# All convolution taps on TensorE, from copies by VectorE and ScalarE, with the mixer's products in a new order

## The chip, the cores and the metric

The kernel runs on one core of a Trainium2 chip. The metric is the device time of one execution in microseconds (us); a run's time is that of the whole program, and the figures of a kernel are the median of its runs. A profile is one execution, recorded instruction by instruction on the five engines: TensorE (PE in the rows, PEld its weight loads), VectorE (DVE), ScalarE (ACT), GpSimd (POOL) and SyncE (SP, which here only issues DMAs).

## The reference: what is computed

A decoder trunk of two layers on 256 tokens of 1024 features, in float32: layer 0 is an FFN, a mixer of pooling and convolution, and an FFN; layer 1 an FFN, a sparse attention, and an FFN; each with RMSNorm ahead and a residual sum behind. What the change touches is the mixer of layer 0, cut here to its core:

```python
proj = h @ ab_w_in[i]                                   # 1024 -> 512 + 512 + 512
u_pool, u_val, u_gate = jnp.split(proj, ab_cuts, axis=-1)
y_pool = pool_mixer(u_pool, pool_w[i], pool_scale[i])   # trailing means over 2, 4, 8, 16 tokens
y_conv = conv_module(u_val, u_gate, conv_w[i], ...)
y = jnp.concatenate([y_pool, y_conv], axis=-1) @ ab_w_out[i]

def conv_module(a, gate, conv_w, conv_b, ln_g, ln_b):
    z = a * jax.nn.sigmoid(gate)
    z = causal depthwise conv of z, width 31, over the tokens, + conv_b
    mu, var = mean and variance of z over the 512 channels
    return jax.nn.silu((z - mu) * lax.rsqrt(var + NORM_EPS) * ln_g + ln_b)
```

Each of the 512 channels has 31 taps of its own: output token t is the sum over n of w[n, channel] * z[t - 30 + n, channel].

## The kernel before, in words

Products of float32 accuracy are made of three fp32r products, high x high, high x low and low x high. So every weight goes through three steps: SP loads it (`raw`, L147), ScalarE rounds it (`hi`, L160), and one engine subtracts (`lo = raw - hi`, L184). `pump(n, eng)` does this for the next n weights of a list that is fixed ahead, in the order of their use; `eng` says which engine subtracts, VectorE unless GpSimd (`pool`) is named, and None shares one weight between the two. A weight of kind "gu" is 1024 x 256 (1 MB, two pieces in every step), one of kind "d" 128 x 1024 (512 KB). Rounded and subtracted weights stand in three buffers of kind "gu" and five of kind "d"; a load is issued when a raw buffer is free.

The program is written out by hand: there is no scheduler, and each engine runs its instructions in the order in which the code issues them. So a line in `mixer_ab` that is moved moves on every engine that it uses.

`mixer_ab` runs after the first FFN, whose tail hands over the normalised, transposed tokens `hT` (the second token tile's transposes are done by `finish_b`, inside `wide`). Features are on the partitions, the 256 tokens in the columns, so a block is 128 channels. It goes through:

- Projections: `wide` makes three weights' products (value and gate of channel blocks 0 to 2), `project` the others one by one: block 3, pooling groups 2 and 3, pooling groups 0 and 1. `wide_sum2` (L716, L717) adds the two halves of a result, `glu` (L505, L506) writes z with 30 zero columns ahead into a tile `keep`.
- The convolution, with taps split: 20 of the 31 are done by TensorE, 11 by VectorE. For TensorE, `shift_z` (L541) copies z into four column shifts: for each of four groups of 32 channels a tile whose 128 partitions hold these 32 channels at four neighbouring tokens. It is 16 copies of 32 partitions for each block, some on ScalarE and the rest on VectorE (`COPIES`). `taps_pe` (L548) then makes 20 products of 128 x 32 weights with 256 columns, four taps in each, from a pack (`wd`). The pack holds each tap's weight on a diagonal of 32; `make_pack` (L524) builds it on GpSimd from the small constants `cpk` and a stacked identity `eye`. `taps_dve` (L567 to L576) is a generator: `conv(n)` issues its next n operations on VectorE, each multiplying z, shifted by one token, with a per-channel weight and adding.
- Pooling: `windows` (L598) sums on GpSimd by doubling, `pool_diff` (L620 to L624) subtracts the token on VectorE, `pool_map` multiplies and splits the result (L638 on ScalarE, L639 on VectorE).
- The channel norm: `mean_mm` on TensorE, `squares` (L673, L674), `variance` (L680, with a power on GpSimd), `spread` (L689), and `swish` for each of two token tiles (L703, L705, L699, L700).
- The output: `out_mm(t, k)` (L349) multiplies pooling block k for token tile t; `tail` multiplies the four convolution blocks, adds the residual, normalises and transposes for the next FFN. `load_gain` reads the norm's gain into the tile that shifts 0 and 2 use as well (`gain`).

Line numbers are those of the kernel before.

## Time and profile before

| what | value |
|---|---|
| median of 3 runs | 1007.56 us (1006.82 to 1009.68) |
| the profiled execution | 1007.73 us |
| its span in the profile | 1006.0 us |
| mean granted clock of TensorE | 0.983 |
| TensorE busy | 967.3 us, 96% of the span |
| VectorE busy | 686.3 us, 68% |
| ScalarE busy | 534.8 us, 53% |
| GpSimd busy | 106.9 us, 11% |

The span is what the profile covers, and the execution's time has 1.73 us around it. Busy time of TensorE counts pipelined products, so 96% is not 96% of its peak. A busy share of the whole span says nothing on one stage: the four FFNs take most of it, and the mixer of layer 0, about 200 to 305 us, is read from the timelines of that stage. In a timeline a row can stand for several instructions one behind the other (xcount), and its length is then that of all of them; what stands in brackets is the engine's idle time before the row and what ended it.

### The profile page before, as it was taken

What the parts mean: (1) busy time and instruction counts of PE and PEld (TensorE: products, weight loads), DVE (VectorE), ACT (ScalarE), POOL (GpSimd) and SP (SyncE); (2) the same over time, 40 slices, a digit from 0 to 9 for tenths busy, and PEclk for the clock granted to TensorE, in tenths of its full rate; (3) what the DMA queues carried; (4) which work ended last, traced back from release to release, by engine and by line L of the source; (5) the groups of instructions that cost most, each with busy time, mean ns of one, the idle gap of its engine ahead of it and who ended that gap; (6) DMA issues with size and microseconds to landing.
All of it is one profiled execution on the core that took longest, in us unless ns stands there. A gap on an engine that the chain in (4) does not pass through costs nothing.

```text
span 1006.0 us, 14588 instructions
## 1 busy us (share of the span) xinstructions
PE 967.3 (96%) x5642; PEld 839.0 (83%) x5642; DVE 686.3 (68%) x1107; ACT 534.8 (53%) x961; POOL 106.9 (11%) x116
## 2 busy tenths in 40 slices
PE   7999999978499999999999999999999999999997
PEld 7888888868279888888888888888889898888885
DVE  6876666689976866665676666657888758666653
ACT  5665555455245755555466555545466646555542
POOL 4000000064520010000000000000344100000000
PEclk9999999998889999999999999999999999999999
DMA  8765555432333756655455555445454526655401
GB/s 334 275 251 188 188 189 189 167 115 85 103 128 110 267 209 235 235 208 188 151 208 223 188 189 189 158 167 188 174 175 158 189 85 230 216 192 192 175 2 42
DMA packets 37460, 179.98 MB, mean 179 GB/s; under 512 B 6352, under 2 KB 6384, under 8 KB 24208
## 3 DMA queue, kind: packets, MB, share of 16 engines
q1 hardware_dynamic: 32400, 169.92, 47.0%
q0 software_dynamic: 4704, 8.88, 2.8%
q8 instruction: 44, 0.72, 0.3%
q10 hardware_dynamic: 288, 0.27, 0.1%
q14 instruction: 24, 0.20, 0.1%
HBM read 177.89 MB, written 4.22 MB: 181 GB/s over the span
## 4 chain that ended last, share of the span: by engine, by line
PE 85%; DVE 10%; issue 2%; ACT 1%; DMA 1%; POOL 0%; SPq 0%; POOLq 0%; DVEq 0%; ACTq 0%
PE g L292 28%; PE g L295 15%; PE a L349 14%; PE b L349 12%; PE g L276 4%; PE g L320 2%; PE g L323 2%; DVE zq L541 1%; PE g L312 1%; DVE odd L569 1%; DVE t L569 1%; DVE lo L184 1%; PE a L323 1%; PE a L320 1%; PE b L869 1%
## 5 line engine op out<-in xcount | busy, mean ns | idle before, releaser
L184 DVE TENSOR_TENSOR lo<-raw,hi 128x1024 fp32r<-128x1024 f32 (+1 forms) x308 | 367.3, 1244 | 53.9 <-ACT hi L160 53.9
L160 ACT CAST hi<-raw 128x1024 fp32r<-128x1024 f32 x320 | 314.9, 1043 | 4.8 <-DMA raw<-in_c_out 2.4
L292 PE MATMUL g<-hT,hi 128*128 128x512 f32 x1248 | 310.7, 391 | 0.8 <-DVE t L335 0.8
L292 PEld LDWEIGHTS g<-hT,hi 128*128 128x128 f32 x1248 | 228.7, 188 | 44.8 <-DVE t L335 1.0
L332 ACT COPY t<-g 128x256 f32<-128x256 f32 x174 | 63.3, 371 | 220.6 <-PE g L295 205.1
L295 PEld LDWEIGHTS g<-hT,lo 128*128 128x128 f32 x1248 | 170.3, 190 | 12.2
L295 PE MATMUL g<-hT,lo 128*128 128x256 f32 x1248 | 174.0, 282 | 0.0
L335 DVE TENSOR_TENSOR t<-g,t 128x256 f32<-128x256 f32 x174 | 71.8, 421 | 137.8 <-ACT t L332 137.8
L349 PE MATMUL a<-hi,kh 128*128 128x512 f32 x208 | 83.3, 401 | 0.1
L349 PE MATMUL b<-hi,kh 128*128 128x512 f32 x208 | 83.0, 399 | 0.0
L349 PE MATMUL a<-lo,kh 128*128 128x512 f32 x208 | 82.3, 396 | 0.0
L349 PE MATMUL a<-hi,kl 128*128 128x512 f32 x208 | 81.3, 391 | 0.7 <-DVE kl L639 0.7
L349 PE MATMUL b<-hi,kl 128*128 128x512 f32 x208 | 81.5, 392 | 0.0
L349 PE MATMUL b<-lo,kh 128*128 128x512 f32 x208 | 81.5, 392 | 0.0
L243 POOL TENSOR_TENSOR sm<-sm,mhalf 128x1 f32<-128x1 f32 x11 | 6.1, 555 | 659.8 <-DVE sm L241 659.8
L398 ACT CAST kh<-t 128x256 fp32r<-128x256 f32 x88 | 35.8, 406 | 57.9 <-DVE t L396 57.9
L399 DVE TENSOR_TENSOR kl<-t,kh 128x256 fp32r<-128x256 f32 x88 | 37.5, 426 | 41.6 <-ACT kh L398 41.6
L276 PE MATMUL g<-hT,hi 128*128 128x256 f32 x320 | 45.9, 300 | 8.6 <-DVE t L717 8.6
L394 ACT ACTIVATE t<-t 128x256 f32<-128x256 f32 x88 | 37.1, 422 | 26.8 <-DVE t L335 26.8
L276 PEld LDWEIGHTS g<-hT,hi 128*128 128x128 f32 x320 | 42.5, 204 | 10.0 <-DVE t L717 9.1
L349 PEld LDWEIGHTS a<-hi,kl 128*128 128x128 f32 x208 | 39.4, 189 | 10.0 <-DVE kl L639 1.1
L349 PEld LDWEIGHTS b<-hi,kl 128*128 128x128 f32 x208 | 39.3, 189 | 8.4
(214 smaller groups left out, 1032.5 us busy)
## 6 DMA issues: line engine op xcount, KB each, us to landing
raw<-in_gu SPq DMA_DIRECT2D x87, 1024.0 KB, 4.8
raw<-in_dn SPq DMA_DIRECT2D x88, 512.0 KB, 5.5
raw<-in_c_qk SPq DMA_DIRECT2D x8, 1024.0 KB, 5.7
raw<-in_ab_in SPq DMA_DIRECT2D x6, 1024.0 KB, 4.9
raw<-in_ab_out SPq DMA_DIRECT2D x8, 512.0 KB, 5.2
raw<-in_c_v SPq DMA_DIRECT2D x8, 512.0 KB, 4.2
raw<-in_c_out SPq DMA_DIRECT2D x8, 512.0 KB, 4.2
eall<-escr POOLq DMA_DIRECT2D x4, 768.0 KB, 17.0
```

Of the source, the lines that this page charges most:

```text
L160: act.copy(hi[:, c], raws[k][:, c])
L184: e.tensor_tensor(lo[:, c], raws[k][:, c], f32(hi[:, c]), op=ALU.subtract)
L276: pe.matmul(dst, wt[:, c, cols], hT[:, c, part, :], start=n == 0, stop=n == len(seq) - 1)
L292: pe.matmul(b, hi[:, c, cols], hT[:, c, 0:2, :], start=c == 0, stop=False, skip_group_check=True)
L295: pe.matmul(b[:, 0:256], lo[:, c, cols], hT[:, c, 0, :], start=False, stop=c == NCH - 1, skip_group_check=True)
L320: pe.matmul(bv[:, :, P:2 * P], w[0][:, c, cs], hT[:, c, 0:2, P:2 * P], start=False, stop=False, skip_group_check=True)
L332: act.copy(t[:m], bv[:, 1, :])
L335: dve.tensor_tensor(dst[:m], bv[:, 0, :], t[:m], op=ALU.add)
L349: pe.matmul(acc, kt[a][:, ts], w[b][:, hs], start=start and n == 0, stop=stop and n == 2)
L394: act.activation(s, gv, AF.Silu)
L398: act.copy(hi, m)
L399: dve.tensor_tensor(lo, m, f32(hi), op=ALU.subtract)
```

## The change

All 31 taps go to TensorE, filled up to 32, so that a pack holds eight rounds of four taps instead of five. The packs are laid out on the host as an input `cpack` (four of 128 x 1024 fp32) and loaded by GpSimd's DMA queue: packs 0 and 1 at the eighth hidden block of the first FFN, 2 and 3 inside the mixer, when the two pack buffers come free. `taps_dve`, `make_pack` and `eye` are gone; one VectorE operation (`taps_out`) adds the bias to TensorE's sum. Six of every 16 shift copies are on ScalarE, ten on VectorE, 284 columns wide instead of 272. Window sums and all subtractions of weights in the mixer are on VectorE; GpSimd keeps memsets, DMA issues and the powers. `wide` uses each of its three results at once and pumps a weight behind each. The lines of `mixer_ab` from the projections on are written in a new order.

```diff
-ROUNDS = 5
-PE_TAPS = 4 * ROUNDS
-DVE_TAPS = TAPS - PE_TAPS
-ZW = 252 + PE_TAPS
-COPIES = (7, 6, 9, 4)
+ROUNDS = 8
+ON_ACT = 6
+ZW = 256 + 4 * (ROUNDS - 1)
...
+    def load_pack(j):
+
+        dg = tpool.tile([P, 4 * ROUNDS, 32], F32, tag="wd", name=nm("wd"), bufs=2)
+        pool.dma_start(dg, d["cpack"][j])
+        packs[j] = dg
+
     def mixer_ab(finish_b, gname):
...
-        def make_pack(j, eng):
-            n = PE_TAPS
-            dg = tpool.tile([P, 32 * PE_TAPS], F32, tag="wd", name=nm("wd"), bufs=3)
...
-                    n_act = COPIES[j]
-                    on_act = (4 * i + q + 1) * n_act // 16 > (4 * i + q) * n_act // 16
+                    on_act = (4 * i + q + 1) * ON_ACT // 16 > (4 * i + q) * ON_ACT // 16
...
-        def taps_dve():
...
+        def taps_out(j):
+            ys[j] = t1()
+            dve.tensor_scalar(ys[j], where[j][:, 0:256], convb[:, j:j + 1], None, op0=ALU.add)
+
...
-                pool.tensor_tensor(s2[:, 2 * n - 1:272], s[:, 2 * n - 1:272],
-                                   s[:, n - 1:272 - n], op=ALU.add)
+                dve.tensor_tensor(s2[:, 2 * n - 1:272], s[:, 2 * n - 1:272],
+                                  s[:, n - 1:272 - n], op=ALU.add)
...
         def use(bvs):
-            wides.append([(bv[:, 0, :], bv[:, 1, :]) for bv in bvs])
-            if len(wides) == 1:
-                glu(0, *[wide_sum2(hi, lo) for hi, lo in wides[0]])
+            val, gt = [wide_sum2(bv[:, 0, :], bv[:, 1, :]) for bv in bvs]
+            glu(len(items), val, gt)
+            items.append(True)
...
-        wide([(weights("gu"), list(zip(two, t)), use) for t in tags], finish_b, False, AHEAD)
-        pump(1, pool)
-        pump(1, pool)
-        conv(14)
+        wide([(weights("gu"), list(zip(two, t)), use) for t in tags], finish_b, True, AHEAD)
         taps_pe(0, "b0")
-        glu(1, *[wide_sum2(hi, lo) for hi, lo in wides[1]])
-        glu(2, *[wide_sum2(hi, lo) for hi, lo in wides[2]])
-        conv(5)
-        pump(1, pool)
-        conv(6)
-        v3 = project("g1")
-        glu(3, *v3)
-        pump(1, dve)
+        taps_out(0)
+        load_pack(2)
+        glu(3, *project("a0"))
         taps_pe(1, "b1")
-        conv(13)
+        taps_out(1)
+        load_pack(3)
         p23 = project("a1")
         windows(2, p23)
-        make_pack(3, pool)
+        taps_pe(2, "b0")
+        taps_out(2)
+        pump(1)
+        g = load_gain(gname)
         pool_diff(2)
-        g = load_gain(gname)
+        taps_pe(3, "g1")
+        mean_mm((0, 1, 2))
+        pump(1)
+        taps_out(3)
         preload(AF.Silu)
         p01 = project("g0")
+        mean_mm((3,))
+        pool_map(2, "g3")
+        squares()
         windows(0, p01)
-        taps_pe(2, "b0")
-        conv(6)
-        pump(1, None)
-        pool_map(2, "g3")
-        taps_pe(3, "g1")
-        pump(1, pool)
+        variance(0, "g1")
+        out_mm(0, 0)
+        out_mm(1, 0)
+        variance(1, "g2")
         pool_diff(0)
-        pump(1, pool)
-        out_mm(0, 0)
-        conv(7)
-        mean_mm((0, 1, 2))
-        pool_map(0, "g3")
+        out_mm(0, 1)
         out_mm(1, 1)
-        conv(5)
-        out_mm(0, 1)
-        out_mm(1, 0)
+        pool_map(0, "g0")
+        spread(0, "g3")
+        spread(1, "g1")
+        pump(1)
+        swish(0)
         out_mm(0, 2)
-        pump(1, None)
-        pump(1, dve)
-        mean_mm((3,))
-        squares()
-        out_mm(1, 2, (1,))
-        out_mm(1, 2, (0,))
-        variance(0, "g1")
-        variance(1, "g3")
+        out_mm(1, 2)
+        pump(1)
         out_mm(0, 3)
-        spread(0, "g1")
-        pump(1, None)
-        swish(0)
-        spread(1, "g0")
+        out_mm(1, 3)
         swish(1)
-        out_mm(1, 3)
+        pump(2)
...
-    pool.tensor_tensor(eye, ident[:, 0:32], ident[:, 32:64], op=ALU.add)
-    for q in (64, 96):
-        pool.tensor_tensor(eye, eye, ident[:, q:q + 32], op=ALU.add)
-    fb = ffn(0, None, "mxn0", first=first)
+    fb = ffn(0, None, "mxn0", first=first, extra=lambda: (load_pack(0), load_pack(1)))
```

The instruction order at three places, of the kernel before first and of the changed kernel second. In the rows, names have buffer numbers; `t` are work tiles, `a`, `b` and `g` PSUM banks, `hi` and `lo` a weight's rounded and subtracted part, `wd` a pack, `gain` and `zq` the shifted copies, `kh` and `kl` the parts of a block for the output product. Line numbers of the changed kernel are its own (its L182 is the subtraction, L528 the shift copy, L535 the taps, L268 a projection, L620 the mean, L587 the pool map).

VectorE, from the first channel block's gate on. Before:

```order
L506 TENSOR_TENSOR keep_1940<-t_399_2083,t_397_2077 128x256
L541 COPY gain_2086<-keep_1940 32x272 x9
L567 TENSOR_SCALAR t_407_2183<-keep_1940,cpk 128x256
L567 TENSOR_SCALAR odd<-keep_1940,cpk 128x256
L569 SCALAR_TENSOR_TENSOR t_407_2183<-keep_1940,cpk,t_407_2183 128x256
L569 SCALAR_TENSOR_TENSOR odd<-keep_1940,cpk,odd 128x256
```

Changed:

```order
L507 TENSOR_TENSOR keep_1940<-t_398_2080,t_396_2074 128x256
L528 COPY gain_2083<-keep_1940 32x284 x10
L182 TENSOR_TENSOR lo_2103<-raw_1710,hi_2100 128x1024 x2
L670 TENSOR_TENSOR t_403_2140<-g_381_1974,t_403_2140 128x256
L670 TENSOR_TENSOR t_404_2143<-g_382_1983,t_404_2143 128x256
L507 TENSOR_TENSOR keep_1943<-t_405_2146,t_403_2140 128x256
L528 COPY zq_2149<-keep_1943 32x284 x5
L528 COPY zq_2150<-keep_1943 32x284 x5
```

Where the eleven taps of block 0 and their sum stood behind the nine copies, the fourth projection's weight (`raw_1710`) is subtracted, which GpSimd did before; the sums and copies of block 1 follow at once.

TensorE, from the last projection on (before), and from the end of the last taps on (changed). Before:

```order
L276 MATMUL g_448_2486<-hT,hi_2276 128x256 x16
L276 MATMUL g_448_2486<-hT,lo_2279 128x256 x8
L276 MATMUL g_448_2486<-hT,hi_2276 128x256 x16
L276 MATMUL g_448_2486<-hT,lo_2279 128x256 x8
L548 MATMUL b_454_2547<-gain_2253,wd_1953 32x256 x20
L634 MATMUL g_459_2583<-t_442_2472,pw 128x256
L634 MATMUL g_459_2583<-t_444_2477,pw 128x256
L548 MATMUL g_464_2594<-zq_2342,wd_2470 32x256 x2
L548 MATMUL g_464_2594<-zq_2343,wd_2470 32x256 x2
```

Changed:

```order
L535 MATMUL g_448_2507<-zq_2331,wd_2383 32x256 x2
L620 MATMUL g_449_2540<-t_419_2274,ones 128x256
L620 MATMUL g_449_2540<-t_426_2381,ones 128x256
L620 MATMUL g_449_2540<-t_439_2487,ones 128x256
L268 MATMUL g_455_2556<-hT,hi_2233 128x256 x16
L268 MATMUL g_455_2556<-hT,lo_2236 128x256 x8
L268 MATMUL g_455_2556<-hT,hi_2233 128x256 x16
L268 MATMUL g_455_2556<-hT,lo_2236 128x256 x8
L620 MATMUL g_449_2540<-t_453_2552,ones 128x256
L587 MATMUL g_456_2606<-t_444_2497,pw 128x256
```

Before, the last projection (`g_448`) is followed by block 2's taps, the first pool map and block 3's taps; now all taps are ahead of it, three mean products stand between, and the last mean product and the pool map follow it.

VectorE, from the second half of `swish` to the tail's first residual sum. Before:

```order
L700 TENSOR_TENSOR kl_2781<-t_522_2808,kh_2780 128x128
L703 TENSOR_TENSOR t_494_2717<-t_494_2717,g_521_2805 128x128
L700 TENSOR_TENSOR kl_2786<-t_523_2811,kh_2785 128x128
L699 CAST kh_2790<-t_524_2814 128x128
L700 TENSOR_TENSOR kl_2791<-t_524_2814,kh_2790 128x128
L700 TENSOR_TENSOR kl_2798<-t_525_2819,kh_2797 128x128
L235 SCALAR_TENSOR_TENSOR x_87<-a_475_2641,x_87 128x512
L235 SCALAR_TENSOR_TENSOR x_88<-a_476_2642,x_88 128x512
```

Changed:

```order
L653 TENSOR_TENSOR kl_2734<-t_513_2789,kh_2733 128x128
L656 TENSOR_TENSOR t_464_2620<-t_464_2620,g_494_2722 128x128
L653 TENSOR_TENSOR kl_2739<-t_514_2792,kh_2738 128x128
L652 CAST kh_2743<-t_515_2795 128x128
L653 TENSOR_TENSOR kl_2744<-t_515_2795,kh_2743 128x128
L653 TENSOR_TENSOR kl_2751<-t_516_2800,kh_2750 128x128
L182 TENSOR_TENSOR lo_2810<-raw_2493,hi_2808 128x1024
L182 TENSOR_TENSOR lo_2817<-raw_2173,hi_2814 128x1024 x2
L227 SCALAR_TENSOR_TENSOR x_86<-a_477_2662,x_86 128x512
```

Between the last `kl` and the residual sum (`x_86` now, `x_87` before) there are now three subtraction pieces: the last output weight (`lo_2810`) and one weight of the next FFN (`lo_2817`).

## Rows read from the trace of the kernel before

**Rows 1.** The page's slices: TensorE's granted clock, 40 slices, tenths of full speed.

```profile
PEclk9999999998889999999999999999999999999999
```

**Rows 2.** TensorE's timeline: start, length, line, out<-in, count, [idle before, releaser].

```profile
204.58 0.66 PE L253 MATMUL b<-ident,h 128*128 128x128 f32 x4 [1.02 <-DVE h L246]
...
218.59 2.37 PE L548 MATMUL b<-gain,wd 128*32 128x256 f32 x40
229.53 3.78 PE L276 MATMUL g<-hT,hi 128*128 128x256 f32 x16 [8.57 <-DVE t L717]
...
239.82 2.18 PE L276 MATMUL a<-hT,hi 128*128 128x256 f32 x16
...
245.67 2.08 PE L276 MATMUL g<-hT,hi 128*128 128x256 f32 x16
...
260.48 1.22 PE L634 MATMUL g<-t,pw 128*128 128x256 f32 x2 [6.59 <-DVE t L624]
...
276.35 1.22 PE L634 MATMUL g<-t,pw 128*128 128x256 f32 x2 [5.77 <-DVE t L624]
...
287.24 1.95 PE L680 MATMUL g<-ones,t 128*128 128x1 f32 x16 [0.26 <-ACT t L674]
...
292.36 0.39 PE L349 MATMUL a<-hi,kh 128*128 128x512 f32 x1
...
304.62 3.98 PE L312 MATMUL g<-hT,hi 128*128 128x256 f32 x32
```

**Rows 3.** Table by stretch: length, TensorE busy, granted clock, DMA share, GB/s.

```profile
222.00:224.00 2.00, 0.00 (x0) 0.99 0.41 66
234.00:236.00 2.00, 2.00 (x18) 0.95 0.00 0
```

**Rows 4.** VectorE's timeline of the mixer stage.

```profile
202.10 2.43 DVE L246 SCALAR_TENSOR_TENSOR h<-x,sm,gain 128x512 f32<-128x512 f32 x2 [0.67 <-POOL sm L243]
...
212.34 0.42 DVE L506 TENSOR_TENSOR keep<-t,t 128x256 f32<-128x256 f32 x1 [0.48 <-ACT t L505]
212.86 2.79 DVE L541 COPY gain<-keep 32x272 f32<-32x272 f32 x9
...
217.01 0.48 DVE L569 SCALAR_TENSOR_TENSOR t<-keep,cpk,t 128x256 f32<-128x256 f32 x1
217.41 2.63 DVE L569 SCALAR_TENSOR_TENSOR odd<-keep,cpk,odd 128x256 f32<-128x256 f32 x1
...
242.16 11.34 DVE L541 COPY zq<-keep 32x272 f32<-32x272 f32 x12
253.53 1.23 DVE L184 TENSOR_TENSOR lo<-raw,hi 128x1024 fp32r<-128x1024 f32 x1
...
269.16 2.62 DVE L620 SCALAR_TENSOR_TENSOR t<-t,t 128x256 f32<-128x256 f32 x1
...
286.51 1.66 DVE L673 TENSOR_TENSOR t<-t,g 128x128 f32<-128x128 f32 x8
...
290.94 0.68 DVE L703 TENSOR_TENSOR t<-t,g 128x128 f32<-128x128 f32 x3 [0.69 <-PE g L689]
...
293.76 0.49 DVE L700 TENSOR_TENSOR kl<-t,kh 128x128 fp32r<-128x128 f32 x2
```

**Rows 5.** GpSimd's timeline of the same stage.

```profile
202.26 4.61 POOL L524 TENSOR_TENSOR wd<-cpk,eye 128x640 f32<-128x640 f32 x3
...
217.03 10.19 POOL L184 TENSOR_TENSOR lo<-raw,hi 128x1024 fp32r<-128x1024 f32 x4 [9.58 <-ACT hi L160]
...
246.50 4.94 POOL L598 TENSOR_TENSOR t<-t 128x271 f32<-128x271 f32 x7
...
269.14 9.45 POOL L184 TENSOR_TENSOR lo<-raw,hi 128x1024 fp32r<-128x1024 f32 x4 [3.87 <-ACT hi L160]
```

**Rows 6.** ScalarE's timeline: its copies for the first shift.

```profile
212.84 3.02 ACT L541 COPY gain<-keep 32x272 f32<-32x272 f32 x7 [0.54 <-DVE keep L506]
```

**Rows 7.** DMA issues, 200 to 310 us: count, KB each, median us to landing.

```profile
gain<-in_f2n POOLq DMA_DIRECT2D x1, 512.0 KB, 4.5
```

More of the change, by code (lines that the diff above doesn't have):

```diff
@@ L206, in tile_trunk @@
     pool.memset(mhalf, -0.5)
-    cpk = cpool.tile([P, 32 + 4 * TAPS], F32, name="cpk")
+    cpk = cpool.tile([P, 32], F32, name="cpk")
     convb, lng, lnb, pscale = (cpk[:, 4 * i:4 * i + 4] for i in range(4))
     rcount = cpk[:, 16:32]
-    convw, packw, o = [], [], 32
-    for j in range(4):
-        convw.append(cpk[:, o:o + DVE_TAPS])
-        packw.append(cpk[:, o + DVE_TAPS:o + TAPS])
-        o += TAPS
-    eye = cpool.tile([P, 32], F32, name="eye")
     escr = dpool.tile([16, 384], F32, name="escr")
@@ L500, in mixer_ab @@
             pool.memset(z[:, 0:30], 0.0)
+            pool.memset(z[:, 286:288], 0.0)
             zs.append(z)
@@ L550, in taps_pe @@
                               stop=m == ROUNDS - 1, skip_group_check=True)
-        def taps_dve():
-            for j in range(4):
-                while j not in ready_z:
-                    yield False
-                z = zs[j]
-                ys[j] = y = t1()
-                sums = [y, odd]
-                for n in range(DVE_TAPS):
-                    acc = sums[n % 2]
-                    zk, wk = z[:, PE_TAPS + n:PE_TAPS + n + 256], convw[j][:, n:n + 1]
-                    if n == 0 and j in where:
-                        dve.scalar_tensor_tensor(acc, zk, wk, where[j][:, 0:256],
-                                                 op0=ALU.mult, op1=ALU.add)
-                        added.add(j)
-                    elif n < 2:
-                        dve.tensor_scalar(acc, zk, wk, None, op0=ALU.mult)
-                    else:
-                        dve.scalar_tensor_tensor(acc, zk, wk, acc, op0=ALU.mult, op1=ALU.add)
-                    yield True
-                dve.scalar_tensor_tensor(y, odd, convb[:, j:j + 1], y, op0=ALU.add, op1=ALU.add)
-                yield True
-                if j not in added:
-                    while j not in where:
-                        yield False
-                    dve.tensor_tensor(y, where[j][:, 0:256], y, op=ALU.add)
-                    added.add(j)
-                    yield True
-        odd = spool.tile([P, 256], F32, name="odd")
-        gen = taps_dve()
-        def conv(n):
-            for _ in range(n):
-                if not next(gen, False):
-                    return
-        for j in range(3):
-            make_pack(j, pool)
+        def taps_out(j):
+            ys[j] = t1()
+            dve.tensor_scalar(ys[j], where[j][:, 0:256], convb[:, j:j + 1], None, op0=ALU.add)
         pw = tpool.tile([P, 512], F32, tag="h", name="pw", bufs=4)
@@ L604, in new_u @@
             u = t15()
-            pool.memset(u[:, 0:16], 0.0)
+            dve.memset(u[:, 0:16], 0.0)
             return u
@@ L1190 @@
     rcount = np.broadcast_to(1.0 / np.arange(1, 17, dtype=np.float32), (P, 16)).astype(np.float32)
+    arrays["cpk"] = np.concatenate(cols + [rcount], axis=1)
+    pack = np.zeros((4, 4, 32, 4, ROUNDS, 32), np.float32)
     for j in range(4):
-        own, n = cw[:, P * j:P * j + P], PE_TAPS
-        cols.append(own[n:].T)
-        cols.append(own[:n].reshape(n // 4, 4, 4, 32).transpose(1, 3, 2, 0).reshape(P, n))
-    arrays["cpk"] = np.concatenate(cols[:4] + [rcount] + cols[4:], axis=1)
+        own = np.zeros((4 * ROUNDS, P), np.float32)
+        own[:TAPS] = cw[:, P * j:P * j + P]
+        own = own.reshape(ROUNDS, 4, 4, 32)
+        for c in range(32):
+            pack[j, :, c, :, :, c] = own[:, :, :, c].transpose(1, 2, 0)
+    arrays["cpack"] = pack.reshape(4, P, 4 * ROUNDS, 32)
     arrays["rel_bias"] = z["rel_bias"]
```

11 lines of the change are left out of this document (2 added, 9 removed).

## The prediction

> **What bounds the kernel now.** I read the page's slices of the span first: TensorE's granted clock shows 9 in every slice but three, slices 10 to 12 of 25 us each, about 226 to 302 us [rows 1]. That is the convolution mixer of layer 0, where nearly all of the change lies, so the rest of the walk is this one stage. TensorE's timeline of the stage comes next: the reader is to see what stands in brackets behind a row. It sat idle for 1.02, 8.57, 6.59 and 5.77 us, each time released by VectorE [rows 2]; smaller waits add some 1.2 us. The clock table then shows what an idle costs behind its end: still 0.99 of full speed at 222 to 224 us, 3 us into the idle that began at 221.0, half speed after that, and full again only at about 234.1, 4.6 us after work had resumed at 229.53 [rows 2, 3]. Work at 1.2 GHz instead of 2.4 lost about 2.3 us there, and the two later idles lost about as much each, some 7 us in all. So VectorE ends last and TensorE waits: of the 101.7 us between the second token tile's transposes and the next FFN's first product (202.9 to 304.62) about 30 are idle time or half speed.
>
> Why VectorE is late stands in its own timeline, read beside GpSimd's. A tap of 256 columns takes 0.48 us at 217.01 and 2.63 at 217.41 [rows 4]; GpSimd began four subtraction pieces at 217.03 and worked on them for 10.19 us [rows 5]. Twelve shift copies took 11.34 us from 242.16, where nine took 2.79 from 212.86; GpSimd's seven window sums ran from 246.50 to 251.4. One operation of pool_diff took 2.62 us at 269.16, and GpSimd had begun at 269.14. The normalisation's two products at 202.10 took 2.43 beside the packs that GpSimd made from 202.26 [rows 4, 5]. VectorE stands nearly still exactly while GpSimd computes.
>
> **The change part by part.** It takes GpSimd's tensor work out of this stage (four packs, 13 subtraction pieces, ten window sums), takes 44 tap operations off VectorE, gives VectorE the subtractions and window sums, gives TensorE 32 taps for each block of 128 channels instead of 20, and puts the products in another order. I lay the new order on the old time axis, with the old durations.
>
> *TensorE, first part.* The wait of 1.02 goes with the packs, so the first three projections end at 218.59 - 1.02 = 217.57. One block's taps cost 2.37 x 32/20 = 3.79; a projection costs 245.67 - 239.82 = 5.85 [rows 2]. In the new order: taps 0 to 221.36, projection to 227.21, taps 1 to 231.00, projection to 236.85, taps 2 to 240.64, taps 3 to 244.43, then the last projection and six 256-column fp32 products (four for the mean, two of the pool map). One such product took 1.22 at half speed, so 0.6 at most at full speed; back to back I take 0.3. That gives 244.43 + 5.85 + 1.8 = 252.1. The extra taps, 4 x 1.42 = 5.7 us, are all on the path.
>
> *Does VectorE keep up?* One projected block costs it two sums and the gate with ScalarE's sigmoid between, 1.8; ten copies at 2.79/9 = 0.31, 4% wider, 3.2; two subtraction pieces at 1.2 (a piece of that size: 1.23), 2.4; and 0.4 in which it waits for ScalarE's rounding. Sum 7.8. The first block's copies end at 215.1 (from 209.3, with 2.6 for its sums), its subtractions at 217.9, the second block's at 225.8, the third's at 233.6 [rows 4]. One output (0.4), the fourth gate (0.4) and ten more copies: 237.7 with its waits for ScalarE. Needed: the third block's copies at 236.85 against 230.9, the fourth's at 240.64 against 237.7. ScalarE's six copies (seven took 3.02 [rows 6]) end before VectorE's ten and cost nothing. Next come seven window sums, which VectorE has not run here. Bounds: 0.42, its sum of two SBUF tiles of 256 columns, and GpSimd's 4.94/7 = 0.71 [rows 4, 5]; I take 0.5, nearest to VectorE's own row: 241.6. With pool_diff, two outputs and three subtraction pieces it reaches 247.5; the last mean product is due at 251. VectorE has 2 to 3 us of slack throughout and is hidden by TensorE.
>
> *TensorE, second part.* From 252.1 short steps follow one another. Two pool-map results are split by ScalarE and VectorE in turn, 4 x 0.5; VectorE starts the squares at 254.2, and the first variance ends 1.7 later (from 286.51 to 287.24 and half of 1.95 [rows 2, 4]): 255.9. TensorE idles for about 2.8 of that. Then 12 output products (at 0.23: the old tail's 48 and two transposes of 0.36 took 304.62 - 292.36), 2.8; a variance, 1.0; 12 more; pool map 0.6; spreads 0.7: 263.7. A wait of 0.5 for the split results and 24 products, 5.5: 269.7.
>
> *A new wait in the tail.* The last two blocks of output weights are now subtracted behind the two swish halves on VectorE. The first swish starts at about 266.8 and takes 3.3 (290.94 to 293.76 + 0.49 [rows 4]): 270.1. With ScalarE's rounding and the subtraction: 271.6. Second swish: 274.9. ScalarE has rounded the last weights by 275.2, VectorE has subtracted them by 276.3. Queued behind that on VectorE are two pieces for the next FFN (2.4), then the residual sum. TensorE is at the tail's first half from 269.7, waits 0.6 for the one and 3.2 and 0.4 for the other, and ends that half at 276.9. Left are 36 products and two transposes, 8.3 + 0.7: 285.9. The old time of that point is 304.62 [rows 2], so 18.7 us are gained. The next FFN's third weights are now subtracted ahead of the second tile's transposed lows; TensorE waits about 0.65 for those. Net 18.05.
>
> A second account: 30 of idle and half speed removed, 5.7 of taps and 8.2 of new waits added, gives 16; the walk stands, and 2 us are its looseness.
>
> *Edits at nothing.* Two packs of 512 KB are loaded at the eighth of the first FFN's 22 hidden blocks, long before use. The other two go out when taps 0 and 1 have freed their buffers, at 221.4 and 231.0. A load of that size landed in 4.5 [rows 7], so they are there at 225.9 and 235.5, needed at 236.85 and 240.64; without that cover each costs what it is late. Behind them on GpSimd's queue stand only a gain load, due some 40 us later, and the rstd powers from 258. The dropped eye operations lie where nobody waits for GpSimd. SP's weight loads keep their order through the eight output blocks and are released no later than before.
>
> **The rivals.** *The clock falls at the new waits.* Idles of 2.8 and 3.2 us follow within 20 us. For: all three old idles of over 5 us ended at half speed. Against: 3 us into the first it was still at 0.99 [rows 3]. Price 2.3 a fall [rows 2, 3]: 992.0 for one, 994.3 for both. Chance 0.18.
>
> *A pack is late.* No row here has a GpSimd DMA issued beside VectorE's copies, so the issue's price there is open. If the fourth pack's issue at 231.0 stands until the copies end at 237.7, it lands at 242.2 and TensorE waits 1.6: 991.3. Chance 0.07. The Trainium skill, "SBUF — State Buffer", section "Who interferes with whom", states such a lock: an fp32 copy within SBUF takes, for the whole instruction, a port pair that GpSimd needs to write a DMA's descriptors. By that rule the sum would be 991.3, by the bare row of the load 989.7; no run here shows which.
>
> *The long VectorE rows were not GpSimd's doing*, and the change does not do what it says. If all 40 copies kept the mean of the slow twelve, 11.34/12 = 0.945 [rows 4], VectorE would lose 40 x 0.63 = 25.2, less 2.9 of slack 22.3: slower than before, 1012. The place is the four series of copies, and it decides from a mean of 0.31 + (18.05 + 2.9)/40 = 0.83 us a copy. With half that excess the time is 999. Against: the starts coincide within 0.4 us in the rows above, and the copies at 212.86, without GpSimd, are fast beside ScalarE's copies of the same tile. Chance 0.03 for slower, 0.04 for the half.
>
> *Less waiting.* If the new waits are hidden (the split chain and the last weights), up to 8.2 more: 981.5 at the bound, 985 in the middle. Chance 0.12.
>
> **How the numbers follow.** The profiled execution took 1007.73 us (span 1006.0, 1.73 around it), close to the median of 1007.56. 1007.73 - 18.05 = 989.7. Chance of that within 3 us: 0.56. The range takes in the less-waiting middle, both clock falls, a late pack, and window sums at 0.71: 983 to 998. About 3 us, 0.3%, is what a measurement of this kernel can tell from no change; of the cases only slow copies come near it. Faster 0.95, same 0.02, slower 0.03.
>
> **What would show it.** In the profile after: no VectorE tap rows; copies of about 0.3 everywhere and no VectorE row of 2 us; taps of 64 TensorE rows in 3.8; the clock full from 200 to 252; TensorE's idles now before the first variance (2.8) and in the tail's first half (3 to 4, released by the weights' halves), and the next FFN's start at about 286 instead of 304.62. Wrong would be a wait for a pack at taps 2 or 3, VectorE as the releaser between 217 and 252, or half speed after the two idles.

## The result, and the profile after

The changed kernel takes 994.94 us (median of 4 runs, 993.01 to 996.05); the kernel before took 1008.05 beside it (4 runs, 1006.82 to 1009.68). The ratio is 0.9866, with an interval of 0.9846 to 0.9886: 13.1 us faster, where 18.05 were predicted. The time lies in the predicted range, 5.2 us above the predicted 989.7. The profiled execution took 993.01 us (span 991.2); it is the fastest of the four, which matters below.

From the page of the changed kernel: busy time of three engines, TensorE's clock in 40 slices, and the shares of the chain that ended last.

```profile
PE 968.1 (98%) x5738; PEld 839.5 (85%) x5738; DVE 657.3 (66%) x1086; ACT 534.0 (54%) x959; POOL 62.9 (6%) x90
...
PEclk9999999999999999999999999999999999999999
...
PE 92%; DVE 3%; issue 2%; ACT 1%; DMA 1%; POOL 0%; SPq 0%; POOLq 0%; DVEq 0%; ACTq 0%
```

The three slices at 8 [rows 1] are gone, GpSimd's busy time fell from 106.9 to 62.9 us, and VectorE's part of the chain, 10% before, is 3%. But a slice is 25 us long and hides what is short. TensorE's timeline of the same stage (start, length, line, out<-in, count, [idle before, releaser]; L535 the taps, L620 the mean, L587 the pool map, L633 the variance, L341 the output products, L304 and L312 the next FFN) answers to [rows 2]:

```profile
217.69 3.66 PE L535 MATMUL b<-gain,wd 128*32 128x256 f32 x64
...
240.25 3.64 PE L535 MATMUL g<-zq,wd 128*32 128x256 f32 x64
...
251.40 1.02 PE L587 MATMUL g<-t,pw 128*128 128x256 f32 x4
255.07 1.05 PE L633 MATMUL g<-ones,t 128*128 128x1 f32 x8 [2.65 <-ACT t L627]
...
260.24 1.13 PE L633 MATMUL g<-ones,t 128*128 128x1 f32 x8
...
273.53 0.50 PE L341 MATMUL a<-lo,kh 128*128 128x512 f32 x1 [0.47 <-DVE lo L182]
...
276.96 0.50 PE L341 MATMUL a<-hi,kh 128*128 128x512 f32 x1 [2.70 <-ACT hi L158]
278.22 0.80 PE L341 MATMUL a<-lo,kh 128*128 128x512 f32 x1 [0.76 <-DVE lo L182]
...
289.24 4.00 PE L304 MATMUL g<-hT,hi 128*128 128x256 f32 x32
...
296.59 1.34 PE L312 MATMUL g<-hT,hi 128*128 128x256 f32 x8 [0.32 <-DVE hT L252]
```

From 200 to 252 us not one row has an idle time in brackets: the old waits of 1.02, 8.57, 6.59 and 5.77 us are gone, and a block's 64 tap instructions (two for each fp32 product) take 3.66. What is left are five waits in brackets: 2.65 before the first variance, 0.47, 2.70 and 0.76 in the tail, 0.32 in the next FFN. The next FFN's first product starts at 289.24 instead of 304.62; predicted was 285.9.

The clock table of the changed kernel shows where most of the missing 3.3 us went (length, then busy time and count of PE, PEld, DVE, ACT and POOL, then TensorE's granted clock, DMA share, GB/s):

```profile
256.00:257.00 1.00, 1.00 (x6) 0.82 (x6) 0.11 (x3) 1.00 (x5) 0.00 (x0) 1.00 0.02 8
257.00:258.00 1.00, 1.00 (x4) 0.84 (x3) 0.00 (x0) 0.00 (x0) 0.00 (x0) 0.60 0.06 16
258.00:259.00 1.00, 1.00 (x4) 0.71 (x4) 0.00 (x0) 0.00 (x0) 0.00 (x0) 0.50 0.00 0
...
260.00:261.00 1.00, 1.00 (x8) 0.91 (x7) 0.25 (x1) 0.00 (x0) 0.00 (x0) 0.69 0.00 0
256.00:264.00 8.00, 8.00 (x34) 6.61 (x34) 2.61 (x14) 1.00 (x5) 1.25 (x2) 0.79 0.01 3
274.00:288.00 14.00, 10.55 (x44) 8.17 (x43) 8.53 (x17) 6.73 (x14) 0.55 (x1) 0.88 0.45 150
```

Work had resumed at 255.07, behind the idle of 2.65 us; 2 us later the clock was still full, then it fell to its lower level (0.50 is 1.2 of 2.4 GHz; 0.60 from 257 to 258 puts the fall at 257.2) and was back at 260.6: 3.4 us at half speed. The same followed the idle of 2.70, from 277.7 to 281.1. The 12 output products between the two variances were predicted at 2.8 us; from the first variance's end (256.12) to the second's start they take 4.1.

VectorE's timeline answers to [rows 4]: shift copies (L528) and window sums (L551).

```profile
211.96 3.18 DVE L528 COPY gain<-keep 32x284 f32<-32x284 f32 x10
...
234.54 3.18 DVE L528 COPY zq<-keep 32x284 f32<-32x284 f32 x10
...
238.37 3.15 DVE L551 TENSOR_TENSOR t<-t 128x271 f32<-128x271 f32 x7
...
260.75 1.34 DVE L551 TENSOR_TENSOR t<-t 128x271 f32<-128x271 f32 x3 [4.64 <-PE g L633]
```

Copies now take 0.3 us everywhere, where the slow twelve took 0.945, and no row of 2 us for one operation is left. The fourth copies end at 237.7, as predicted to the tenth, and the seven window sums take 0.45 each.

### The profile page after: what moved, and what is told of

Read it like the earlier page. It is cut to its first block, busy times and chain, and to the rows that moved or that the text cites. A ratio compares the mean times of both kernels' runs of the same rounds, so it can differ in the third digit from the quotient of the medians.

```text
span 991.2 us, 14724 instructions
## 1 busy us (share of the span) xinstructions
PE 968.1 (98%) x5738; PEld 839.5 (85%) x5738; DVE 657.3 (66%) x1086; ACT 534.0 (54%) x959; POOL 62.9 (6%) x90
## 4 chain that ended last, share of the span: by engine, by line
PE 92%; DVE 3%; issue 2%; ACT 1%; DMA 1%; POOL 0%; SPq 0%; POOLq 0%; DVEq 0%; ACTq 0%
PE g L284 29%; PE g L287 15%; PE a L341 14%; PE b L341 13%; PE g L268 4%; PE g L312 2%; PE g L315 2%; PE g L304 2%; PE a L268 1%; PE b L535 1%; DVE lo L182 1%; PE a L315 1%; PE a L312 1%; PE b L811 1%; DVE keep L957 1%
## 5 line engine op out<-in xcount | busy, mean ns | idle before, releaser
L182 DVE TENSOR_TENSOR lo<-raw,hi 128x1024 fp32r<-128x1024 f32 (+1 forms) x319 | 380.4, 1243 | 56.3 <-ACT hi L158 56.3
L284 PEld LDWEIGHTS g<-hT,hi 128*128 128x128 f32 x1248 | 228.7, 188 | 44.8 <-DVE t L327 1.0
L341 PE MATMUL a<-hi,kh 128*128 128x512 f32 x208 | 83.4, 401 | 2.8 <-ACT hi L158 2.7
L341 PE MATMUL a<-lo,kh 128*128 128x512 f32 x208 | 82.8, 398 | 1.2 <-DVE lo L182 1.2
L341 PE MATMUL b<-hi,kh 128*128 128x512 f32 x208 | 82.3, 396 | 0.0
L341 PE MATMUL a<-hi,kl 128*128 128x512 f32 x208 | 81.8, 393 | 0.0
L341 PE MATMUL b<-hi,kl 128*128 128x512 f32 x208 | 81.5, 392 | 0.0
L341 PE MATMUL b<-lo,kh 128*128 128x512 f32 x208 | 81.5, 392 | 0.0
L341 PEld LDWEIGHTS a<-hi,kh 128*128 128x128 f32 x208 | 39.6, 191 | 10.0 <-ACT hi L158 3.1
L341 PEld LDWEIGHTS a<-hi,kl 128*128 128x128 f32 x208 | 39.5, 190 | 9.0 <-DVE kl L592 0.2
L341 PEld LDWEIGHTS b<-hi,kl 128*128 128x128 f32 x208 | 39.3, 189 | 8.3
L341 PEld LDWEIGHTS b<-hi,kh 128*128 128x128 f32 x208 | 39.4, 189 | 8.2
```

Of the source, the lines that this page charges most:

```text
L182: e.tensor_tensor(lo[:, c], raws[k][:, c], f32(hi[:, c]), op=ALU.subtract)
L284: pe.matmul(b, hi[:, c, cols], hT[:, c, 0:2, :], start=c == 0, stop=False, skip_group_check=True)
L341: pe.matmul(acc, kt[a][:, ts], w[b][:, hs], start=start and n == 0, stop=stop and n == 2)
```

## The experiments

The theory was: VectorE ended last because GpSimd's tensor work stretched its operations and because it had 44 taps to do; with both gone TensorE is full but for short idles, and these cost their length and, as the profile after shows, a stretch at half speed. The rivals: GpSimd's share was nothing or everything; the pack loads cost something; the idles cost only their length. The stage below is the time from the first taps to the next FFN's first product: 86.0 us before (304.62 - 218.59), 71.55 after. (The old wait of 1.02 us, which goes as well, lies ahead of it.) It is a sharper measure than the run's time, since the time at which the stage begins scatters by up to 5 us (last section). The kernel before was run again beside each version, and its median there lay between 1006.49 and 1010.13 us; so ratios compare two versions better than their medians do.

**GpSimd's tensor work alone taken out of the kernel before.** The taps, the packs and the order stay.

```diff
-                pool.tensor_tensor(s2[:, 2 * n - 1:272], s[:, 2 * n - 1:272],
+                dve.tensor_tensor(s2[:, 2 * n - 1:272], s[:, 2 * n - 1:272],
...
-        pump(1, pool)
+        pump(1)
...
-        pump(1, None)
+        pump(1)
```

> The kernel before with one edit: inside the mixer, the 13 subtraction pieces and the ten window sums that GpSimd did are done by VectorE; taps stay 20 on TensorE and 11 on VectorE, the packs are still made on GpSimd, the order of the products is the old one. Theory (GpSimd's tensor work holds VectorE back): VectorE gains back some 27 us of stretched rows and takes on 13 x 1.2 + 10 x 0.45 = 20 us, so the time falls by about 7 us, to 998 to 1004, and no VectorE row of 2 us stands beside GpSimd except at the packs. Rival (VectorE is late by its taps, and the long rows are not GpSimd's doing): 20 us of added work on the engine that is waited for, 1020 to 1028.

Measured: 1001.88 us (1001.27 to 1004.19), ratio 0.9927 [0.9911, 0.9943]. VectorE's timeline of this kernel (L541 copies, L598 window sums):

```profile
246.15 3.65 DVE L541 COPY zq<-keep 32x272 f32<-32x272 f32 x12
...
256.25 3.15 DVE L598 TENSOR_TENSOR t<-t 128x271 f32<-128x271 f32 x7
```

Its TensorE:

```profile
230.12 3.72 PE L276 MATMUL g<-hT,hi 128*128 128x256 f32 x16 [6.99 <-DVE t L717]
...
260.06 2.08 PE L634 MATMUL g<-t,pw 128*128 128x256 f32 x4 [6.10 <-DVE t L624]
...
271.55 1.30 PE L634 MATMUL g<-t,pw 128*128 128x256 f32 x4 [1.95 <-DVE t L624]
```

The twelve copies that took 11.34 us [rows 4] take 3.65, though VectorE now also makes the subtractions and the window sums. So the long rows were GpSimd's doing; the rivals (1012 in the prediction, 1020 to 1028 here) are refuted. But TensorE still waits 6.99, 6.10 and 1.95 us for VectorE, and the stage is 80.8 us (in the slowest of the four executions, which is the profiled one). This part of the change is worth some 7 of its 13 us.

**The new order without GpSimd's work, but with 11 taps of each block back on VectorE.**

```diff
-ROUNDS = 8
+ROUNDS = 5
...
-            dve.tensor_scalar(ys[j], where[j][:, 0:256], convb[:, j:j + 1], None, op0=ALU.add)
+            for n in range(DVE_TAPS):
...
+                    dve.scalar_tensor_tensor(acc, zk, wk, acc, op0=ALU.mult, op1=ALU.add)
```

> The changed kernel with taps split as before: 20 of 31 taps on TensorE (packs of five rounds, copies 272 wide), 11 on VectorE at the place of each block's output; no tensor work on GpSimd, order as changed. Theory (moving taps is the second part of the gain): TensorE has 5.7 us less, VectorE about 18 us more with 2 to 3 us of slack, so TensorE waits for it and the time is 1003 to 1010. Rival (the whole gain is GpSimd's absence and the order): within 2 us of the changed kernel's 994.9, or faster by the 5.7 us of products.

Measured: 1007.74 us (1002.31 to 1009.63), ratio 0.9978 [0.9961, 0.9995]; stage 84.2. The table by stretch (VectorE's busy time is the third behind the length, after PE and PEld):

```profile
230.00:240.00 10.00, 6.73 (x67) 4.00 (x66) 9.66 (x25) 3.54 (x10) 0.54 (x1) 0.93 0.47 159
240.00:250.00 10.00, 4.74 (x40) 3.08 (x38) 9.68 (x28) 4.67 (x6) 0.00 (x0) 0.84 0.00 0
250.00:260.00 10.00, 6.99 (x34) 6.82 (x35) 9.90 (x24) 0.00 (x0) 0.00 (x0) 0.55 0.26 84
```

Two waits of its TensorE (L635 the mean, L648 the variance):

```profile
253.01 1.22 PE L635 MATMUL g<-t,ones 128*128 128x256 f32 x2 [7.31 <-DVE t L556]
...
266.60 1.05 PE L648 MATMUL g<-ones,t 128*128 128x1 f32 x8 [2.65 <-ACT t L642]
```

VectorE is busy 29.2 of 30 us, and TensorE waits for it. The profiled execution took 1002.31 us, the fastest of ten, so the typical stage is longer than 84.2. The new order is made for short work on VectorE; with the taps there it gains next to nothing, and it is some 5 us slower than the old order with the same split in the run above (ratios 0.9978 and 0.9927). So 5.7 us more products on TensorE bought 11 us by the ratios: the order and the place of the taps belong together. The old order with all taps on TensorE was not run, so what the order alone is worth there stays open.

**Subtractions of three projection weights back on GpSimd**, the rest as changed.

```diff
-                pump(1)
+                pump(1, eng)
...
-        wide([(weights("gu"), list(zip(two, t)), use) for t in tags], finish_b, True, AHEAD)
+        wide([(weights("gu"), list(zip(two, t)), use) for t in tags], finish_b, True, AHEAD, pool)
```

> The changed kernel with one edit: the three weights that are subtracted behind the three first projections (six pieces, 7 us of VectorE) are subtracted by GpSimd instead. Theory (GpSimd holds VectorE back): VectorE loses work and gets slower all the same; copies and sums beside GpSimd's pieces take up to 2.5 us, TensorE waits at taps 1 to 3, and the time rises by 5 to 15 us to 1000 to 1010. Rival (only VectorE's own amount of work counts): no slower than the changed kernel, 993 to 996.

Measured: 1004.08 us (1003.15 to 1004.28), ratio 0.9943 [0.9928, 0.9958]; stage 82.6. The time is as the theory has it, but the trace says that most of it came another way. TensorE's wait:

```profile
245.15 5.05 PE L535 MATMUL b<-gain,wd 128*32 128x256 f32 x64 [7.99 <-DVE t L551]
```

And GpSimd's rows (L182 subtractions, L493 the loads of packs):

```profile
234.06 4.78 POOL L182 TENSOR_TENSOR lo<-raw,hi 128x1024 fp32r<-128x1024 f32 x2 [4.27 <-issue]
238.78 1.13 POOL L493 DMA_DIRECT2D wd<-in_cpack  x2
```

The taps at 245.15 read pack 2, and both packs' loads were issued together from 238.78 on, right behind GpSimd's last subtraction; in the changed kernel they go out at 221.69 and 231.25. The row names VectorE's window sums as releaser, which these taps don't read; the two loads took 6.6 us to land (median), and the first landing is about when the taps begin. So this run mixes two prices, and two more runs part them: both leave out the loads of packs 2 and 3, the one without and the other with the subtractions on GpSimd.

```diff
-        load_pack(2)
+        packs[2] = packs[0]
...
-        load_pack(3)
+        packs[3] = packs[1]
```

> The changed kernel, but blocks 2 and 3 use packs 0 and 1 again, so the two packs that are loaded inside the mixer are left out (the weights of those two blocks are not the right ones; every instruction of the engines stays). Theory (the issues on GpSimd's queue beside VectorE's copies cost nothing; they stood 0.53 us each and nobody waited): 994 to 996, stage (first taps to the next FFN's first product) 71 to 72.2 against 71.55. Rival (the issues or the 1 MB of loads slow VectorE's copies): at least 1 us less, copies below 0.29 us each.

> The same without the two packs, and the subtractions of the three projections' weights back on GpSimd, as in e2_subs_on_gpsimd, but now no load can stand behind them. Theory (GpSimd's tensor work slows VectorE by itself, through what the two share): VectorE's fourth copies take 5 to 6 us for ten instead of 3.2 and end at about 241 to 242, although 7 us of work were taken off VectorE; two rows of 2.6 us for one operation beside GpSimd's; TensorE waits 1 to 4 us at the fourth block's taps or the mean; stage 73 to 77, time 996.5 to 1000.5. Rival (all of e2's loss was the packs standing behind the subtractions on GpSimd's queue): no wait of TensorE between 200 and 250 us, stage 71 to 72.2, time as e7_two_packs within 0.7.

Measured: 994.38 us (991.03 to 994.78, ratio 0.9841 [0.9816, 0.9867]) without, and 994.05 (993.37 to 994.81, ratio 0.9849 [0.9832, 0.9866]) with the subtractions on GpSimd. The first is the changed kernel's time within its interval: the two loads cost nothing. Its stage, 74.5 us, misses the expected 71 to 72.2, because half speed behind its two idles lasted longer than in the first profile of the changed kernel (see the changed kernel once more, below). Of the second, VectorE's timeline:

```profile
218.56 2.62 DVE L507 TENSOR_TENSOR keep<-t,t 128x256 f32<-128x256 f32 x1 [0.48 <-ACT t L506]
221.28 3.18 DVE L528 COPY zq<-keep 32x284 f32<-32x284 f32 x10
...
235.79 5.86 DVE L528 COPY zq<-keep 32x284 f32<-32x284 f32 x10
```

GpSimd's:

```profile
216.16 4.74 POOL L182 TENSOR_TENSOR lo<-raw,hi 128x1024 fp32r<-128x1024 f32 x2 [12.70 <-ACT hi L158]
...
234.11 4.81 POOL L182 TENSOR_TENSOR lo<-raw,hi 128x1024 fp32r<-128x1024 f32 x2 [4.26 <-issue]
```

And TensorE's taps of blocks 2 and 3:

```profile
237.16 3.66 PE L535 MATMUL b<-gain,wd 128*32 128x256 f32 x64
240.63 4.78 PE L535 MATMUL g<-zq,wd 128*32 128x256 f32 x64
```

On VectorE the theory holds. A gate of 0.43 us takes 2.62, from 218.56 to 221.18, when GpSimd's pair of pieces from 216.16 had ended at 220.90, and the copies behind it are fast again; ten copies of 3.18 take 5.86. GpSimd worked 14.3 us on what VectorE does in 7.1 (three times 2.36), and VectorE lost 2 x 2.2 + 2.7 = 7.1 us meanwhile, so nothing was gained on it, and its fourth copies end at 241.7 instead of 238.1 without GpSimd's work. On TensorE the expected price did not come (996.5 to 1000.5 us were expected): the fourth taps take 4.78 instead of 3.64, a wait of 1.1, because VectorE's slack of 2 to 3 us hid the rest. The time is the same as without; the stage is 74.2 against 74.5 us, but half speed behind its first idle held 3.4 us against 6.8, which is 1.7 us less work lost, so the contention cost TensorE 1.1 to 1.3. In the run with pack loads the stage was 11 us longer than the changed kernel's: 8.0 are the wait for pack 2 and 1.4 the half speed behind it (64 tap instructions in 5.05 instead of 3.66). So nearly all of its loss came from loads that stood behind tensor work on GpSimd's queue and the clock behind that wait, and little from the engines' contention. The theory, which gave the whole price to contention, was wrong in that, and this last expectation missed.

**The idles filled.** Six 256-column fp32 products of constants, whose result nobody reads, go ahead of the first variance and as many into the tail's first half. In the trace each product is two instructions.

```diff
+        fb = bank("b1")
+        for _ in range(6):
+            pe.matmul(fb[:, 0:256], ident, pw[:, 0:256], start=True, stop=True)
         squares()
```

> The changed kernel with six added 256-column fp32 products that nobody reads in each of the two idle places of TensorE: ahead of the first variance, and in the tail's first half ahead of the last block of output weights. They last about 2.6 us, as long as the idle time there, so they add nothing by themselves. Theory (each of these idles of 2.7 us is followed by 3.6 us at half speed, which cost 1.8 us each and was missing in the forecast): the clock stays full, and the time falls by 3 to 4 us to 991 to 992. Rival (the clock falls for another reason, or the time is set by VectorE behind it): within 1 us of 994.9.

Measured: 989.69 us (988.51 to 990.11), ratio 0.9800 [0.9786, 0.9815]; stage 68.7; the clock is full throughout the stage. The first six products in TensorE's timeline:

```profile
252.10 2.75 PE L715 MATMUL b<-pw,ident 128*128 128x256 f32 x12
```

And the clock table behind either place (length, TensorE's busy time and count, granted clock, DMA share, GB/s):

```profile
254.00:258.00 4.00, 3.94 (x22) 1.00 0.02 6
258.00:262.00 4.00, 4.00 (x23) 1.00 0.00 0
...
276.00:280.00 4.00, 3.48 (x15) 1.00 0.61 160
```

Useless work makes the kernel 5.3 us faster by the medians (6.7 by the ratios), to 1.3 below the theory's range. So half speed behind the idles is real time, and it is more than the 3 us that the profiled execution of the changed kernel shows.

**The changed kernel once more**, to see whether that execution was typical.

> The changed kernel itself, once more, with a profile. Theory (how long TensorE stays at half speed behind the same idle differs from one execution to the next): the idles are again 2.65 and 2.70 us within 0.1, and the stretch at half speed behind at least one of them differs by over 1 us from the profiled 3.5 and 3.7; 993 to 997, stage 71.5 to 74.6. Rival (the two missing loads of e7_two_packs made its stretches longer): 3.5 and 3.7 again within 0.3, stage 71.3 to 71.8.

Measured: 994.71 us, stage 74.45 (292.46 - 218.01) where the first profile had 71.55. Its TensorE at the two idles:

```profile
255.38 1.86 PE L633 MATMUL g<-ones,t 128*128 128x1 f32 x8 [2.65 <-ACT t L627]
...
278.74 0.53 PE L341 MATMUL a<-hi,kh 128*128 128x512 f32 x1 [2.70 <-ACT hi L158]
```

The two stretches of its clock table:

```profile
256.00:264.00 8.00, 8.00 (x30) 6.76 (x31) 1.72 (x10) 1.31 (x6) 0.00 (x0) 0.62 0.01 3
274.00:288.00 14.00, 10.10 (x30) 7.20 (x29) 8.41 (x17) 6.43 (x13) 0.00 (x0) 0.76 0.42 150
```

The idles are the same to 0.05 us; behind them the clock is 0.62 and 0.76 where it was 0.79 and 0.88. Half speed held about 6.8 us each time here, from 255.2 and from 279.1 (8 us x 0.38 of lost clock is 3.0 us, and 0.3 more before 256), 3.4 in the first profile; less what lay in idle time, a fall cost 3.0 to 3.3 us here and 1.4 to 1.7 there. The run without two packs shows the long stretches as well (0.61 and 0.76 in the same two windows), so the loads don't decide it. The length differs from execution to execution, and the profiled one, the fastest of its four, had two short ones.

**The idles taken away by order.** Three versions: the tail alone (the weights of the last output blocks pumped earlier, window sums behind the second variance), the first idle alone (a pool map ahead of the projection, 12 output products ahead of the variance), and both, which also puts the last window sums and `pool_diff` ahead of the variances and spreads the subtractions anew.

The tail:

```diff
         taps_out(3)
+        pump(1)
         preload(AF.Silu)
...
         squares()
-        windows(0, p01)
         variance(0, "g1")
         out_mm(0, 0)
         out_mm(1, 0)
+        pump(1)
         variance(1, "g2")
+        windows(0, p01)
         pool_diff(0)
...
         swish(1)
-        pump(2)
```

> The changed kernel with only the pumps moved: the last three output weights are subtracted one step earlier each (behind the first output products, behind the spreads, between the two swish halves), and the next FFN's second weight behind the last block's output, so that none stands behind the second swish; the window sums go behind the second variance, for which they wait anyway. Theory (the wait in the tail's first half, 0.47 + 2.70 + 0.76 us, and 1.8 us of half speed behind it, are the late subtractions): 5 us less, 989 to 991, and TensorE without an idle of over 0.5 us from 266 to the end of the tail. Rival (swish itself or the norm behind it sets the end): less than 2 us gained, the idle moved to the transposes.

The first idle:

```diff
         taps_out(3)
+        pool_map(2, "g3")
         preload(AF.Silu)
...
-        pool_map(2, "g3")
         squares()
         windows(0, p01)
-        variance(0, "g1")
         out_mm(0, 0)
         out_mm(1, 0)
+        variance(0, "g1")
```

> The changed kernel with the first pool map ahead of the last projection and the first 12 output products ahead of the first variance instead of behind it. Theory (the idle of 2.65 us and 1.8 us of half speed behind it come from the chain of short steps, which other products can cover): 3 to 4.5 us less, 990.5 to 992. Rival (the chain of squares, window sums and pool_diff is as long as before and only moves the wait to the second pool map): within 1.5 us of 994.9.

Both (the window sums' copies go into a tile `keep`, so that they wait for no square):

```diff
         taps_out(3)
+        pool_map(2, "g3")
+        pump(1)
...
         mean_mm((3,))
-        pool_map(2, "g3")
-        squares()
-        windows(0, p01)
-        variance(0, "g1")
         out_mm(0, 0)
         out_mm(1, 0)
-        variance(1, "g2")
+        us = window_copies(p01, keep)
+        squares()
+        window_adds(0, us)
         pool_diff(0)
+        variance(0, "g1")
+        variance(1, "g3")
+        pool_map(0, "g0")
         out_mm(0, 1)
+        pump(1)
+        spread(0, "g2")
+        spread(1, "g1")
+        swish(0)
         out_mm(1, 1)
-        pool_map(0, "g0")
-        spread(0, "g3")
-        spread(1, "g1")
-        pump(1)
-        swish(0)
         out_mm(0, 2)
         out_mm(1, 2)
-        pump(1)
+        pump(2)
...
         swish(1)
-        pump(2)
...
-        return tail(accs, kts[4:8], [weights("d") for _ in range(4)], 1.0, g, (0, 0))
+        return tail(accs, kts[4:8], [weights("d") for _ in range(4)], 1.0, g, (1, 0))
```

> Both edits and one more: the last window sums and pool_diff come ahead of the variances, in tiles that are free by then, and two weights of the next FFN are subtracted where VectorE is idle. Theory (TensorE bounds the whole stage once its two waits are covered): about 10 us less than the changed kernel, 983 to 986, the clock full throughout the stage. Rival (the edits move the wait to the swish or the norm): no better than the better of the two single edits, 989 to 991.

| version | median, us | ratio to before | stage, us |
|---|---|---|---|
| changed | 994.94 | 0.9866 [0.9846, 0.9886] | 71.55 and 74.45 |
| idles filled | 989.69 | 0.9800 [0.9786, 0.9815] | 68.68 |
| no idle in the tail | 988.12 | 0.9784 [0.9765, 0.9804] | 66.63 |
| no first idle | 989.51 | 0.9793 [0.9776, 0.9809] | 68.37 |
| neither | 982.76 | 0.9731 [0.9717, 0.9746] | 62.20 |

What idle is left in each of the three, from TensorE's timelines; first the version without an idle in the tail:

```profile
254.71 1.05 PE L633 MATMUL g<-ones,t 128*128 128x1 f32 x8 [2.64 <-ACT t L627]
```

The version without the first idle:

```profile
274.36 0.71 PE L341 MATMUL a<-hi,kh 128*128 128x512 f32 x1 [2.70 <-ACT hi L158]
```

The one without either:

```profile
278.00 0.66 PE L245 MATMUL a<-ident,h 128*128 128x128 f32 x4 [1.52 <-DVE h L238]
```

And its row of the table by stretch for the whole stage:

```profile
200.00:280.00 80.00, 78.47 (x691) 67.00 (x690) 62.37 (x147) 48.84 (x97) 4.67 (x16) 1.00 0.44 149
```

Each idle goes as planned and the other stays as it was. The tail's three waits, 3.9 us in all, and the first of 2.65 are worth 6.8 and 5.4 us by the medians (8.3 and 7.4 by the ratios), about their length and one fall. All three versions came out 0.2 to 1.0 us below the lower end of what the theory gave, which had its price of a fall from the short stretches of the first profile. Without both idles the clock is 1.00 over the whole stage and TensorE is busy 78.5 of 80 us. That version beats both kernels: 27 us less than before, 12 less than the changed one.

## Why the prediction was right, and where its number was not

- **The waits for VectorE go, because GpSimd stood in its way and because of the taps.** Right in direction and in size: copies of 0.3 us, no VectorE row of 2 us, and a kernel before without GpSimd's work in which the same copies took 3.65 us instead of 11.34. The Trainium skill, "SBUF — State Buffer", section "Who interferes with whom", calls what the two engines share an exclusive lock: a VectorE instruction with two SBUF inputs contends with a GpSimd instruction that reads SBUF, and the order of issue decides which of them blocks. The trace agrees: the gate of 0.43 us took 2.62 and ended 0.28 us after GpSimd's piece.
- **TensorE's first part.** Taps 3.66 (3.79 predicted), projections 5.95 (5.85), end at 252.4 (252.1). Right.
- **VectorE keeps up.** Its subtractions end at 218.0, 225.8 and 233.6, predicted 217.9, 225.8 and 233.6; copies end at 237.7. The window sums at 0.45 us each were taken at 0.5. The second window sums wait 4.64 us for a buffer that the second variance frees (the row at 260.75), which the walk had not seen; no one waited for them.
- **The pack loads at nothing.** Right. GpSimd issued them at 221.69 and 231.25 in 0.53 us each, right when the buffers came free, and no taps waited:

```profile
221.69 0.53 POOL L493 DMA_DIRECT2D wd<-in_cpack  x1 [18.60 <-PE b L535]
231.25 0.53 POOL L493 DMA_DIRECT2D wd<-in_cpack  x1 [9.03 <-PE b L535]
```

The first stood beside the fp32 copies of block 1 (219.75 to 222.98), and it took no longer than the second; the two loads landed in 3.8 us at the median. By the rule that the prediction quoted from the same section of the Trainium skill, such copies can starve a GpSimd DMA of its descriptors; these rows show no stall of the size that was priced, the measurement decides, and the rival of 991.3 falls. (The issue at 231.25, which the rival named, met a subtraction on VectorE and no copies.) The cover was real, though: where the loads were issued 17 and some 8 us later, the stage was 11 us longer.

- **The new waits.** Predicted 2.8 before the variance and 0.6, 3.2 and 0.4 in the tail; measured 2.65 and 0.47, 2.70 and 0.76. The sum was 7.0 and is 6.58. Right. The wait for the transposed lows was put at 0.65 and is 0.32.
- **The step that failed** is the one behind these waits: I priced each at its length, because 3 us into an old idle the clock was still at 0.99 [rows 3]. That row only shows the clock during an idle, in which it costs nothing; it does not show what comes after the work has resumed. In the changed kernel the fall came 2.1 and 0.7 us after the idle's end. Without the falls the walk holds: the predicted stage is 285.9 - 217.57 = 68.3 us; the profiled 71.55 less 1.7 and 1.4 is 68.4, 74.45 less 3.3 and 3.0 is 68.1, and the kernel with its idles filled, where the clock did not fall, has 68.7. That is closer than the walk's terms deserve: the first part ends 0.3 us late and the waits are 0.4 us shorter, and a product's step of 0.23 was read a little low (the interval it cites gives (304.62 - 292.36 - 0.72) / 48 = 0.24), under 1 us over the walk.
- **So the rival that happened** is "the clock falls at the new waits", at both: 994.3 was its time, 994.94 the median. Its price of 2.3 a fall, from the old trace, lies between the 1.4 to 1.7 and the 3.0 to 3.3 measured, so that its sum came so close is partly luck. A chance of 0.18 was too small: all three old idles had ended so, and the one row against it did not speak of the same thing.
- **The other rivals.** Slow copies without GpSimd are refuted by the kernel before without GpSimd's work. Less waiting did not come by itself; it had to be ordered, and was then worth 12 us.

## What to carry to other kernels

When VectorE holds the bound, look beside its long rows for what GpSimd does at the same microsecond; moving that work onto VectorE itself can make VectorE faster (twelve copies in 3.65 us instead of 11.34 here). A DMA issue that something soon waits for should not stand behind tensor work on GpSimd's queue: here that was a wait of 8.0 us. Once TensorE is full, price an idle of some 2 to 3 us that is left at its length and a stretch of half speed behind it (1.4 to 3.3 us here, nothing in one case), and give it independent products by order: here two such idles were worth 12 us. Judge the price of an idle by rows behind its end, not by the clock within it.

## What the runs showed of the hardware that was not expected

- **The same idle is followed by half speed of very different length.** Behind 2.65 and 2.70 us it held 3.4 us each in one execution, 6.8 in another of the same kernel. In the version with split taps an idle of 2.65 us (the row at 266.60) was followed by none: its clock is full from there to 280 us.

```profile
260.00:280.00 20.00, 16.98 (x91) 14.13 (x91) 10.63 (x38) 6.16 (x18) 1.25 (x2) 1.00 0.10 40
```

In the other versions that keep one or both idles half speed held 3.4 or 6.8 us as well, never a length between. What decides between these was not found; I leave it open.

- **The program's start scatters, it seems for the same reason.** TensorE idles 4.00 us up to 12.07 in the changed kernel and 2.93 up to 11.48 in the one with split taps. The table by stretch, 10 to 15 us, of the changed kernel:

```profile
10.00:15.00 5.00, 2.93 (x15) 2.94 (x16) 5.00 (x11) 1.14 (x4) 3.13 (x2) 0.66 1.00 418
```

And of the one with split taps:

```profile
10.00:15.00 5.00, 3.52 (x29) 3.50 (x30) 5.00 (x14) 2.80 (x9) 3.12 (x2) 1.00 1.00 419
```

The clock there is 0.66 in the one and 1.00 in the other, and the first taps begin at 217.69 and 215.96. The other profiles with the changed order fit this: the first taps begin at 217.3 to 218.1 us where half speed near the start held 3.4 us, and at 218.8 and 219.6 in the two where it held 6.8. No run changed the start, so this is read from rows and not tried. In all the profiles they begin between 215.96 and 220.76, so part of the spread between runs is made long before the mixer. That is why the stage is compared above beside the run.

- **A GpSimd subtraction of 128 x 1024 takes 2.4 us** beside VectorE's work, where VectorE's own takes 1.2, and VectorE lost as much as it was spared (7.1 for 7.1 us).
